# Reordering VectorE's work between the first two weight pairs of a fused decoder trunk's last matrix product, and forming one operand's low parts by an adding DMA

## The chip, the cores and the metric

The kernel runs on one core of a Trainium2 chip. The metric is the device time of one execution in microseconds (us). Before the change three runs took 1341.61, 1343.89 and 1345.63 us; their median is 1343.89 us. One execution was also recorded by the hardware profiler. Times within it are counted from the start of its span.

## The reference

One decoder layer over 1024 tokens of width 1024, all in float32. The change lies in the last part, the gated MLP's down projection, its residual and the final norm.

```python
def conv_ffn(xn, w_up, conv_w, conv_b, w_down):
    u = xn @ w_up
    upad = jnp.pad(u, ((0, 0), (CONV_WIDTH - 1, 0), (0, 0)))
    c = conv_b
    for j in range(CONV_WIDTH):
        c = c + upad[:, j:j + S] * conv_w[j]
    gate, val = jnp.split(c, 2, axis=-1)
    return (jax.nn.silu(gate) * val) @ w_down        # 2816 -> 1024

def reference(...):
    ...                                              # norm, two attentions, merge, residual
    xn = rmsnorm(x, norm_ffn_w[l])
    x = x + conv_ffn(xn, w_up[l], conv_w[l], conv_b[l], w_down[l])
    return rmsnorm(x, norm_final_w)
```

## The kernel before

**Three products for one.** Every float32 operand is split into a high part (a copy rounded to the format that TensorE reads, `F32R`) and a low part (the operand minus its high part). A product is made of high x high, high x low and low x high. ScalarE makes the high part (`nc.scalar.copy`), VectorE the low part (`tensor_tensor ... subtract`). For weights the tiles are `wh`/`wl` and `sh`/`sl`, for activations a tile `h<slot>` holds both parts side by side. `split` (L832) and `parts_h` (L1041) do this for activations.

**Down projection (`down`, L1110).** The hidden width 2816 is 22 chunks of 128. The first 6 go through a plain product (L1159). The next 8 and the last 8 are two groups, and each group is multiplied by a scheme with seven block products instead of eight: output rows m and m + 4 form a pair (four pairs, m = 0..3), the tokens are two halves of 512, and the operands are single blocks or sums of blocks of the weights (A11, A12, A22, S1 to S4) and of the activations (B11, B21, B22 and the sums T1 to T4). One block product (`product`, L906) is 12 TensorE instructions: four chunks k times three parts. Results gather in PSUM banks, tags `d` and `y`, four of each, and VectorE adds them into the output tile `x3` (`x` in the profile, `col(m, hf)` in the code).

**The second group, around the change.** The loop over m at L1279 makes for each pair, in this order on TensorE:

- P1 = A11 x B11 into a bank `y`. VectorE adds the bank into `col(m, 0)` (L1285) and leaves it as it is, since P6 and P7 gather on top of it.
- P2 = A12 x B21 into a bank `d`, added by `evac` (L1260), which also squares and weighs the finished block on ScalarE for the final norm (L1263, L1267).
- P7 = S3 x T3 of the pair before (`seventh`, L1275), onto that pair's `y`.
- P4 = A22 x T4 into a bank `d`, subtracted at L1292.
- P6 = S2 x T2 onto `y`, added at L1294. It may be written only after L1285 has read P1.

After the loop come `fifth` (with T1) and `third` (with B22), whose weight sums were stored in HBM (`sd`) and are read back, and then the final norm in pieces (`last_norm`, L1347).

**Weights of a pair** come by `second_pair` (L138): two loads on SyncE's queue into three rotating `raw` buffers, four sums on GpSimd (L148 to L151), a store of two of them, and three splits (L157), of A11/A12 and of S2/S3 (128x1024 each) and of A22 (128x512). `next_w(n)` hands out the next pair and makes sure that n are under way.

**Operands of the second group.** The list `more` (L1216) holds the steps in order: B11, B21, T4, T2, the four tiles `box` for the norm's sums, T3, T1, B22, four steps (k = 0..3) each. `prepare(n)` takes the next n steps. `read` loads a raw row block `hr` from HBM (L1034) and splits it; `ready` splits a difference that was formed earlier (`diffs`, L1201). Slots are `h14` to `h17` for T4, `h21, h25, h1, h5` for T2, `h20, h24, h0, h4` for T3, `h7, h9, h11, h13` for T1, `h6, h8, h10, h12` for B22.

A scheduler places the instructions on each engine's queue mostly in the order of the code; `tc.issue_after(i)` asks for a place behind instruction i on its engine. Each engine then works its queue in order.

Of the kernel before, what the change touches and what calls it, by code (L numbers as in the profile page):

```python
# [10 lines left out]
F32 = mybir.dt.float32  # L11
F32R = mybir.dt.float32r
AF = mybir.ActivationFunctionType
ALU = mybir.AluOpType
# [3 lines left out]
P = 128  # L18
# [4 lines left out]
H2 = 512  # L23
# [8 lines left out]
N2 = N1 + 8  # L32
# [12 lines left out]
class Trunk:  # L45
    def __init__(self, tc, ins, out):
        self.tc, self.nc = tc, tc.nc
        (self.xT, self.w_in, self.w_br, self.w_mix, self.w_up, self.w_dn,
         self.vecs_d, self.bias_d) = ins
        self.out = out  # L50
        self.uid = 0
        self.stores = []
        self.uw = self.w22 = self.behind = None
        self.pin, self.after = False, None
        self.hs, self.defer, self.late = {}, [], []

    def name(self, s):
# [80 lines left out]
    def second_pair(self, src, m):  # L138

        nc = self.nc  # L140
        raws = []
        for x in src:
            raws.append(self.tl(self.wp, [P, 8, P], "raw", bufs=RAW))
            nc.sync.dma_start(raws[-1], x)
        g, v = (r.rearrange("p (k a) c -> p a k c", a=2) for r in raws)
        sa, sb = (self.tl(self.sfp[0], [P, 2, 4, P], self.sfp[1]) for _ in range(2))
        tt = nc.gpsimd.tensor_tensor
        tt(sa[:, 0], v[:, 0], v[:, 1], ALU.add)  # L148
        tt(sb[:, 0], sa[:, 0], g[:, 0], ALU.subtract)
        tt(sb[:, 1], g[:, 0], v[:, 0], ALU.subtract)  # L150
        tt(sa[:, 1], g[:, 1], sb[:, 0], ALU.subtract)  # L151
        nc.sync.dma_start(self.sd[m], sa.rearrange("p a k c -> p (a k) c"))
        ops = {}
        for pool, h, l, x, names in ((self.wp, "wh", "wl", g, ("A11", "A12")), (self.uw, "sh", "sl", sb, ("S2", "S3")), (self.wp, "wh", "wl", v[:, 1:2], ("A22",))):
            hi = self.tl(pool, [P, len(names), 4, P], h, F32R)
            lo = self.tl(pool, [P, len(names), 4, P], l, F32R)
            self.made = nc.scalar.copy(hi, x), nc.vector.tensor_tensor(lo, x, hi.bitcast(F32), ALU.subtract)  # L157
            for i, name in enumerate(names):
                ops[name] = hi[:, i], lo[:, i]
        return ops  # L160

    def load_raw(self, src, nk):
# [875 lines left out]

        return self.tl(self.hp if i < HP else self.hpb, [P, 2, H2], f"h{i}", dt)

    def parts_h(self, src, i=None):  # L1041

        if i is None:
            i = self.nh % (HP + HPB)
            self.nh += 1
        h = self.slot(i, F32R)
        return self.split(h[:, 0], h[:, 1], src)

    def load_h(self, j, hf, eng=None):
# [60 lines left out]
    def down(self):  # L1110

        nc, tc = self.nc, self.tc
        with ExitStack() as ctx:
# [7 lines left out]
            tt = nc.vector.tensor_tensor  # L1121
            bank = lambda n: self.tl(psD, [P, H2], "dy"[n])
            x3 = xp.tile([P, KC, T], F32, name="x3")
            col = lambda m, hf: x3[:, m, hf * H2:(hf + 1) * H2]
# [20 lines left out]
            n = N1 // 2  # L1145
            for i, (m, c) in enumerate(self.pieces):
# [3 lines left out]
                w = [v[:, i % 2 * n:i % 2 * n + n] for v in w2]  # L1150
                lo = self.lo
                for hf in range(2):
# [3 lines left out]
                    for q, j in enumerate(js):  # L1156
                        h, l = self.hs[hf, j]
# [16 lines left out]
                if c == 1:  # L1174

                    for hf in range(m < 4, 2):
                        x = col(m, hf)
# [3 lines left out]
            for m in range(4):  # L1181
                wh, wl = self.next_w()
                y, ps = bank(1), pss[m, 0]
# [26 lines left out]
            def ready(n, k, i):  # L1210
                self.B["2" + n, k] = self.parts_h(raws[k][("T1", "T3", "T4", "T2").index(n)], i)

            def read(n, k, o, hf, i):
                self.B["2" + n, k] = self.parts_h(self.raw_h(N2 + 2 * k + o, hf), i)

            box = []  # L1216
            more = [lambda k=k: read("B11", k, 0, 0, old("T1", k)) for k in range(4)]
            more += [lambda k=k: read("B21", k, 1, 0, old("T2", k)) for k in range(4)]
            more += [lambda k=k: ready("T4", k, base + 8 + k) for k in range(4)]
            more += [lambda k=k: ready("T2", k, old("T4", k)) for k in range(4)]  # L1220
            more += [lambda: box.append(self.tl(self.hrp, [P, H2], "hr")) for _ in range(4)]
            more += [lambda k=k: ready("T3", k, old("T3", k)) for k in range(4)]
            more += [lambda k=k: ready("T1", k, base + 2 * k + 1) for k in range(4)]
            more += [lambda k=k: read("B22", k, 1, 1, base + 2 * k) for k in range(4)]

            def prepare(n):
                for _ in range(min(n, len(more))):
                    more.pop(0)()
# [3 lines left out]
            for m, y in enumerate(ys):  # L1232
                w = self.next_w()
# [5 lines left out]
                i = tt(col(m, 1), col(m, 1), y, ALU.add)  # L1239
# [7 lines left out]
                i = tt(col(m + 4, 0), col(m + 4, 0), ps, ALU.subtract)  # L1247
# [2 lines left out]
                self.product(y, w["S3"], "T3", first=False, skip=True)  # L1250
                for hf in range(2):
                    tt(col(m + 4, hf), col(m + 4, hf), y, ALU.add)
            prepare(20)
            q = H2 // 2
            seen = []

            def evac(ps, m, hf, a=0, b=H2, last=False):

                x = x3[:, m, hf * H2 + a:hf * H2 + b]
                tt(x, x, ps, ALU.add)  # L1260
                sum_ = box[hf][:, a:b]
                sq = box[2 + len(seen) % 2][:, a:b] if hf in seen else sum_
                self.square = nc.scalar.activation(sq, x, AF.Square)  # L1263
                if hf in seen and not last:
                    tt(sum_, sum_, sq, ALU.add)
                seen.append(hf)
                weigh = lambda: nc.scalar.mul(x, x, self.vecs[:, C_NO + m:C_NO + m + 1])  # L1267
                if last:
                    return sq, weigh
                weigh()  # L1270
# [3 lines left out]
            def seventh(m):  # L1274
                self.product(ys[m], ws[m]["S3"], "2T3", first=False, skip=True)  # L1275
                evac(ys[m], m + 4, 0)
                tt(col(m + 4, 1), col(m + 4, 1), ys[m], ALU.add)

            for m in range(4):  # L1279
                w = self.next_w()  # L1280
                ws.append(w)
                y, ps = bank(1), bank(0)
                ys.append(y)
                self.product(y, w["A11"], "2B11", skip=True, low_last=True)
                tt(col(m, 0), col(m, 0), y, ALU.add)  # L1285
                self.product(ps, w["A12"], "2B21")
                evac(ps, m, 0)
                if m:
                    seventh(m - 1)
                ps = bank(0)  # L1290
                self.product(ps, w["A22"], "2T4")
                tt(col(m + 4, 0), col(m + 4, 0), ps, ALU.subtract)  # L1292
                self.product(y, w["S2"], "2T2", first=False, skip=True)
                tt(col(m, 1), col(m, 1), y, ALU.add)  # L1294
                with ExitStack() as queue:
                    for i in self.made:
                        queue.enter_context(tc.issue_after(i.ins))
                    prepare(4 if m else 8)
            seventh(3)
            assert not more  # L1300
            tail = self.last_norm(psD, [box[0]], x3, 0, 0, H2, ((0, 2, nc.vector), (6, 8, nc.gpsimd), (2, 4, nc.vector), (4, 6, nc.vector)))
# [145 lines left out]
```

## Time and profile before

| | |
|---|---|
| median of three runs | 1343.89 us |
| the profiled execution | 1342.84 us |
| its span, first to last instruction | 1340.6 us |
| TensorE (PE) busy | 1319.9 us, 98% |
| VectorE (DVE) busy | 1069.3 us, 80% |
| ScalarE (ACT) busy | 621.2 us, 46% |
| GpSimd (POOL) busy | 497.0 us, 37% |
| mean granted TensorE clock | 0.997 |
| second group, 1247 to 1304 us: TensorE | 54.1 us of 57 busy |
| second group: VectorE | 53.7 us of 57 busy |

PE, DVE, ACT and POOL are the engines; SPq is SyncE's queue of DMA issues. A row of a timeline is start, duration, engine, line, operation, the tile written and the tiles read, their shapes and a count of like instructions that follow each other; in brackets stands the idle time before it and who ended it. Matmuls overlap, so the distance between two starts is what one costs, not its duration. `out<-in` names leave out buffer numbers, so all `h` slots read alike.

### The profile page before, as it was taken

The numbers are of one execution on the slowest core, as the hardware profiler recorded it, in microseconds if no ns is written. First come the engines' busy times: TensorE is split into PE (matmuls) and PEld (weight loads), VectorE is DVE, ScalarE is ACT, GpSimd is POOL, SyncE is SP. The second block draws the span as 40 slices with busy tenths as digits, with TensorE's granted clock in tenths as the row PEclk, the third lists the DMA queues.
The fourth block names the chain that finished last, engine by engine and source line by source line (L and its number), as shares of the span: only waits on it lengthen the run. The fifth ranks groups of instructions, "written<-read, shape, count | busy, mean of one in ns | idle before, by whom it ended". The sixth has DMA issues, their size and how long they took to land.

```text
span 1340.6 us, 17301 instructions
## 1 busy us (share of the span) xinstructions
PE 1319.9 (98%) x6264; PEld 1097.0 (82%) x6264; DVE 1069.3 (80%) x1605; ACT 621.2 (46%) x1019; POOL 497.0 (37%) x365
## 2 busy tenths in 40 slices
PE   8999999999999999999999999999999999999997
PEld 6888888888888777878888888888888888888787
DVE  8847775289889876465678999999999997978985
ACT  9432232276667765333444443444443444323454
POOL 0336553001102124651446555655565510215422
PEclk9999999999999999999999999999999999999998
DMA  7423443876553235334432222222222229671333
GB/s 258 145 107 143 156 158 141 246 182 186 144 135 124 97 119 203 141 110 157 126 110 95 78 95 79 94 68 90 90 85 80 85 82 337 214 263 63 112 124 126
DMA packets 63045, 182.64 MB, mean 136 GB/s; under 512 B 6896, under 2 KB 15216, under 8 KB 62960
## 3 DMA queue, kind: packets, MB, share of 16 engines
q1 hardware_dynamic: 51504, 164.13, 37.5%
q10 hardware_dynamic: 11456, 17.41, 3.6%
q8 instruction: 49, 0.80, 0.3%
q14 instruction: 36, 0.29, 0.1%
HBM read 130.66 MB, written 50.86 MB: 135 GB/s over the span
## 4 chain that ended last, share of the span: by engine, by line
PE 87%; POOL 4%; DVE 4%; DMA 3%; ACT 1%; issue 1%; POOLq 0%; SPq 0%; ACTq 0%; DVEq 0%
PE t L920 13%; PE t L921 13%; PE t L922 13%; PE g L209 3%; PE t L914 3%; PE g L210 3%; PE g L211 3%; PE sc L636 3%; PE y L1159 2%; PE d L1159 2%; DMA gr<-gd 2%; PE sc L211 2%; PE sc L209 2%; PE sc L210 2%; PE d L920 2%; PE d L921 2%
## 5 line engine op out<-in xcount | busy, mean ns | idle before, releaser
L1089 ACT ACTIVATE c<-us,vecs 128x512 f32<-128x512 f32 x80 | 61.3, 780 | 133.2 <-POOL us L1083 129.2
L1091 DVE SCALAR_TENSOR_TENSOR c<-us,vecs,c 128x512 f32<-128x512 f32 x160 | 110.4, 747 | 8.6 <-ACT c L1089 8.5
L1083 POOL TENSOR_TENSOR us<-us,rstd 128x1024 f32<-128x1024 f32 x38 | 99.7, 2643 | 4.5 <-DVE us L469 2.4
L128 DVE TENSOR_TENSOR sl<-sf,sh 128x1024 fp32r<-128x1024 f32 x62 | 87.6, 1415 | 11.5 <-ACT sh L127 11.5
L127 ACT CAST sh<-sf 128x1024 fp32r<-128x1024 f32 x62 | 63.3, 1048 | 60.2 <-PE t L921 43.7
L176 DVE TENSOR_TENSOR wl<-raw,wh 128x1024 fp32r<-128x1024 f32 (+2 forms) x46 | 55.7, 1210 | 31.8 <-ACT wh L174 20.2
L128 DVE TENSOR_TENSOR wl<-raw,wh 128x1024 fp32r<-128x1024 f32 (+1 forms) x35 | 76.3, 2180 | 3.7 <-ACT wh L127 3.6
L103 POOL TENSOR_TENSOR sf<-rv 128x512 f32<-128x512 f32 x30 | 41.3, 1378 | 100.9 <-DVE sl L128 57.8
L174 ACT CAST wh<-raw 128x1024 fp32r<-128x1024 f32 (+2 forms) x46 | 46.1, 1001 | 61.8 <-PE sc L210 30.5
L209 PE MATMUL g<-xh,wh 128*128 128x512 f32 x176 | 70.6, 401 | 0.1
L211 PE MATMUL g<-xh,wl 128*128 128x512 f32 x176 | 70.3, 400 | 0.0
L210 PE MATMUL g<-xl,wh 128*128 128x512 f32 x176 | 70.3, 399 | 0.0
L108 POOL TENSOR_TENSOR sf<-raw,rv 128x512 f32<-128x512 f32 x30 | 40.7, 1358 | 65.3 <-DVE sl L128 65.3
L619 POOL MEMSET aT<- 128x128 f32 x32 | 6.2, 206 | 151.6 <-PE t L665 101.3
L640 DVE CUSTOM_DVE_ANT_0 L<-sc,bias 128x128 f32<-128x128 f32 (+7 forms) x64 | 47.7, 751 | 17.0 <-PE sc L636 13.7
L641 ACT ACTIVATE L<-L,sm 128x128 f32<-128x128 f32 (+7 forms) x64 | 49.6, 778 | 20.0 <-DVE sm L640 17.3
L794 POOL TENSOR_TENSOR gr<-gr,rstd 128x1024 f32<-128x1024 f32 x16 | 40.6, 2540 | 42.5 <-DMA gr<-gd 42.3
L1093 ACT ACTIVATE c<-c 128x512 f32<-128x512 f32 x40 | 24.0, 599 | 60.7 <-DVE c L1091 60.7
L128 DVE TENSOR_TENSOR wl<-rv,wh 128x512 fp32r<-128x512 f32 x30 | 49.3, 1642 | 3.5 <-ACT wh L127 3.5
L636 PE MATMUL sc<-u,u 128*128 128x512 f32 (+2 forms) x192 | 49.8, 358 | 0.0
L211 PE MATMUL sc<-mh,wl 128*128 128x512 f32 x126 | 49.1, 390 | 0.5 <-DVE wl L176 0.5
L209 PE MATMUL sc<-mh,wh 128*128 128x512 f32 x126 | 49.0, 389 | 0.0
(527 smaller groups left out, 4400.3 us busy)
## 6 DMA issues: line engine op xcount, KB each, us to landing
u<-qd SPq DMA_DIRECT2D x72, 256.0 KB, 6.6
raw<-in_w_in SPq DMA_DIRECT2D x25, 512.0 KB, 4.2
raw<-in_w_up SPq DMA_DIRECT2D x23, 512.0 KB, 3.5
hr<-hd SPq DMA_DIRECT2D x46, 256.0 KB, 4.9
hd<-c SPq DMA_DIRECT2D x22, 512.0 KB, 2.6
rv<-in_w_up SPq DMA_DIRECT2D x21, 512.0 KB, 3.5
raw<-in_w_down SPq DMA_DIRECT2D x19, 512.0 KB, 4.2
gr<-gd SPq DMA_DIRECT2D x16, 512.0 KB, 3.7
```

The costliest lines, as they stand in the source:

```text
L127: i = nc.scalar.copy(hi, src)
L128: j = nc.vector.tensor_tensor(lo, src, hi.bitcast(F32), ALU.subtract)
L209: nc.tensor.matmul(ps, wh[:, kc + o, :], ah, start=first and n == 0, stop=False)
L210: nc.tensor.matmul(ps, wh[:, kc + o, :], al, start=False, stop=False)
L211: nc.tensor.matmul(ps, wl[:, kc + o, :], ah, start=False, stop=last and n == len(kcs) - 1)
L636: nc.tensor.matmul(sc[:, lo + n0:lo + n1], qs, k[c][part][:, n0:n1], start=part == 0, stop=part == 1)
L920: nc.tensor.matmul(ps, ah[:, k, :], bh, start=first and n == 0, stop=False, skip_group_check=skip)
L921: nc.tensor.matmul(ps, ah[:, k, :], bl, start=False, stop=False, skip_group_check=skip)
L922: i = nc.tensor.matmul(ps, al[:, k, :], bh, start=False, stop=last and n == len(ks) - 1, skip_group_check=skip)
L1083: (nc.vector if j == 0 else nc.gpsimd).tensor_tensor(u[:, 2:], u[:, 2:], self.rstd, ALU.mult)
L1089: nc.scalar.activation(c, u[:, o + 2:o + 2 + H2], AF.Identity, bias=self.vecs[:, C_CB + m:C_CB + m + 1], scale=col(m, 2))
L1091: nc.vector.scalar_tensor_tensor(c, u[:, o + k:o + k + H2], col(m, k), c, ALU.mult, ALU.add)
```

## The change

Four edits, all in the second group:

- `prepare(20)` ahead of the loop becomes `prepare(16)`: T2's splits no longer stand ahead of the loop. The `box` tiles are taken ahead of T2. Inside the loop, for m = 0, T2's splits are issued behind the addition of P1 (`issue_after`).
- The second pair is asked for (`ahead(1)`) behind that addition too, and its splits are queued behind it (`self.later`).
- After each pair four steps are prepared instead of eight after the first: T3, T1 and B22 follow pairs 0, 1 and 2.
- B22's low parts are formed in another way: ScalarE copies the high part and then multiplies it by -1 into the low part's place, and a DMA issued by GpSimd adds the raw rows `hr` onto it.

```diff
@@ second_pair
-            self.made = nc.scalar.copy(hi, x), nc.vector.tensor_tensor(lo, x, hi.bitcast(F32), ALU.subtract)
+            with self.tc.issue_after(self.later.ins) if self.later is not None else nullcontext():
+                self.made = nc.scalar.copy(hi, x), nc.vector.tensor_tensor(lo, x, hi.bitcast(F32), ALU.subtract)
...
+        self.later = None
         return ops
@@ parts_h
-    def parts_h(self, src, i=None):
+    def parts_h(self, src, i=None, adding=False):
...
+        if adding:
+            self.nc.scalar.copy(h[:, 0], src)
+            self.nc.scalar.mul(h[:, 1], h[:, 0].bitcast(F32), -1.0)
+            self.nc.gpsimd.dma_start(h[:, 1], src, accum_op=ALU.add)
+            return h[:, 0], h[:, 1]
         return self.split(h[:, 0], h[:, 1], src)
@@ down
-                self.B["2" + n, k] = self.parts_h(self.raw_h(N2 + 2 * k + o, hf), i)
+                self.B["2" + n, k] = self.parts_h(self.raw_h(N2 + 2 * k + o, hf), i, n == "B22")
...
+            more += [lambda: box.append(self.tl(self.hrp, [P, H2], "hr")) for _ in range(4)]
             more += [lambda k=k: ready("T2", k, old("T4", k)) for k in range(4)]
-            more += [lambda: box.append(self.tl(self.hrp, [P, H2], "hr")) for _ in range(4)]
...
-            prepare(20)
+            prepare(16)
...
-                w = self.next_w()
+                w = self.next_w(2 if m else 1)
...
-                tt(col(m, 0), col(m, 0), y, ALU.add)
+                i = tt(col(m, 0), col(m, 0), y, ALU.add)
+                if m == 0:
+                    with tc.issue_after(i.ins):
+                        prepare(4)
+                    self.later = i
+                    self.ahead(1)
...
-                    prepare(4 if m else 8)
+                    prepare(4)
```

What it does to the queues, first on VectorE at the start of the second group. Before, from T4's last low part (`h17`): T2's low parts, the second pair's A11/A12 (`wl_1903`) and S2/S3 (`sl_1905`), the addition of P1 (L1285), A22 (`wl_1907`), and then the additions of P2 and P4.

```order
L834 TENSOR_TENSOR h17_1889_10945<-h13_1817_10508,h17_1889_10945 128x512
L834 TENSOR_TENSOR h21_1890_10948<-h7_1811_10496,h21_1890_10948 128x512
L834 TENSOR_TENSOR h25_1891_10951<-h9_1813_10500,h25_1891_10951 128x512
L834 TENSOR_TENSOR h1_1892_10954<-h11_1815_10504,h1_1892_10954 128x512
L834 TENSOR_TENSOR h5_1893_10957<-h13_1817_10508,h5_1893_10957 128x512
L157 TENSOR_TENSOR wl_1903_10976<-raw_1898_10964,wh_1902_10975 128x1024
L157 TENSOR_TENSOR sl_1905_10980<-c_1901_10969,sh_1904_10979 128x1024
L1285 TENSOR_TENSOR x3_9784<-x3_9784,y_1908_10987 128x512
L157 TENSOR_TENSOR wl_1907_10984<-raw_1899_10966,wh_1906_10983 128x512
L1260 TENSOR_TENSOR x3_9784<-x3_9784,d_1909_10988 128x512
L1292 TENSOR_TENSOR x3_9784<-x3_9784,d_1910_11017 128x512
```

After the change, from the same row (lines are a few numbers higher, L1293 is the addition of P1, L1307 that of P6):

```order
L837 TENSOR_TENSOR h17_1889_10945<-h13_1817_10508,h17_1889_10945 128x512
L1293 TENSOR_TENSOR x3_9784<-x3_9784,y_1894_10952 128x512
L837 TENSOR_TENSOR h21_1896_10967<-h7_1811_10496,h21_1896_10967 128x512
L837 TENSOR_TENSOR h25_1897_10970<-h9_1813_10500,h25_1897_10970 128x512
L837 TENSOR_TENSOR h1_1898_10973<-h11_1815_10504,h1_1898_10973 128x512
L837 TENSOR_TENSOR h5_1899_10976<-h13_1817_10508,h5_1899_10976 128x512
L159 TENSOR_TENSOR wl_1905_10991<-raw_1900_10979,wh_1904_10990 128x1024
L159 TENSOR_TENSOR sl_1907_10995<-c_1903_10984,sh_1906_10994 128x1024
L159 TENSOR_TENSOR wl_1909_10999<-raw_1901_10981,wh_1908_10998 128x512
L1268 TENSOR_TENSOR x3_9784<-x3_9784,d_1895_10953 128x512
L1305 TENSOR_TENSOR x3_9784<-x3_9784,d_1910_11017 128x512
L1307 TENSOR_TENSOR x3_9784<-x3_9784,y_1894_10952 128x512
```

The addition of P1 moved from behind six rows (T2 and the second pair) to ahead of them, and the addition of P6 moved ahead of T3's first low parts.

TensorE at the same place, before, from the last instruction of P4 (`d_1910`): six instructions of the second pair's P1 (`y_1929`), then P6 of the first pair (`y_1908`).

```order
L922 MATMUL d_1910_11017<-h17_1889_10945,wl_1866_10823 128x512
L914 MATMUL y_1929_11091<-h18_1871_10898,wh_1902_10975 128x512 x2
L914 MATMUL y_1929_11091<-h22_1873_10903,wh_1902_10975 128x512 x2
L914 MATMUL y_1929_11091<-h26_1875_10908,wh_1902_10975 128x512 x2
L920 MATMUL y_1908_10987<-h21_1890_10948,sh_1863_10818 128x512
L921 MATMUL y_1908_10987<-h21_1890_10948,sh_1863_10818 128x512
L922 MATMUL y_1908_10987<-h21_1890_10948,sl_1864_10819 128x512
```

After, from the same row; the first pair's bank is now `y_1894`, and the second pair's P1 begins behind all twelve instructions of P6:

```order
L925 MATMUL d_1910_11017<-h17_1889_10945,wl_1866_10823 128x512
L923 MATMUL y_1894_10952<-h21_1896_10967,sh_1863_10818 128x512
L924 MATMUL y_1894_10952<-h21_1896_10967,sh_1863_10818 128x512
L925 MATMUL y_1894_10952<-h21_1896_10967,sl_1864_10819 128x512
L923 MATMUL y_1894_10952<-h25_1897_10970,sh_1863_10818 128x512
L924 MATMUL y_1894_10952<-h25_1897_10970,sh_1863_10818 128x512
L925 MATMUL y_1894_10952<-h25_1897_10970,sl_1864_10819 128x512
```

P6 moved ahead of the second pair's P1.

ScalarE around B22 (`h6, h8, h10, h12`), before:

```order
L833 CAST h6_1933_11168<-hr_1932_11166 128x512
L833 CAST h8_1935_11173<-hr_1934_11171 128x512
L833 CAST h10_1937_11178<-hr_1936_11176 128x512
L833 CAST h12_1939_11183<-hr_1938_11181 128x512
L157 CAST wh_1944_11197<-raw_1940_11186 128x1024
```

After, from the split of the fourth pair's A22 (`wh_1940`) to the first weights that are read back (`wh_1954`):

```order
L159 CAST wh_1940_11185<-raw_1933_11168 128x512
L1051 CAST h6_1947_11268<-hr_1946_11266 128x512
L1051 CAST h8_1949_11274<-hr_1948_11272 128x512
L1052 ACTIVATE h6_1947_11268<-h6_1947_11268 128x512
L1052 ACTIVATE h8_1949_11274<-h8_1949_11274 128x512
L1051 CAST h10_1951_11280<-hr_1950_11278 128x512
L1051 CAST h12_1953_11286<-hr_1952_11284 128x512
L1052 ACTIVATE h10_1951_11280<-h10_1951_11280 128x512
L1052 ACTIVATE h12_1953_11286<-h12_1953_11286 128x512
L177 CAST wh_1954_11290<-raw_1942_11189 128x1024
```

B22's high parts moved behind the fourth pair's weights, and four multiplications by -1 (L1052) joined them.

GpSimd at the end of the weight sums, after; before, the four DMA rows are not there:

```order
L152 TENSOR_TENSOR c_1934_11170<-raw_1932_11166,c_1935_11171 128x512
L1053 DMA h6_1947_11268<-hr_1946_11266 128x512
L1053 DMA h8_1949_11274<-hr_1948_11272 128x512
L1053 DMA h10_1951_11280<-hr_1950_11278 128x512
L1053 DMA h12_1953_11286<-hr_1952_11284 128x512
L232 TENSOR_TENSOR rs_1969_11438<-ms_1968_11436,mhalf_78 128x4
```

The four adding DMAs stand between the last weight sum and the first power of the final norm. SyncE's queue keeps its order.

More of the change, by code (lines that the diff above doesn't have):

```diff
@@ L156, in second_pair @@
             lo = self.tl(pool, [P, len(names), 4, P], l, F32R)
-            self.made = nc.scalar.copy(hi, x), nc.vector.tensor_tensor(lo, x, hi.bitcast(F32), ALU.subtract)
+            with self.tc.issue_after(self.later.ins) if self.later is not None else nullcontext():
+                self.made = nc.scalar.copy(hi, x), nc.vector.tensor_tensor(lo, x, hi.bitcast(F32), ALU.subtract)
             for i, name in enumerate(names):
                 ops[name] = hi[:, i], lo[:, i]
+        self.later = None
         return ops
```

## The prediction

> **What bounds the kernel now.** I read the page first, then TensorE's waits and the chain of waits in the stretch that the change touches, then the timelines of the engines there.
>
> ```profile
> span 1340.6 us, 17301 instructions
> PE 1319.9 (98%) x6264; PEld 1097.0 (82%) x6264; DVE 1069.3 (80%) x1605; ACT 621.2 (46%) x1019; POOL 497.0 (37%) x365
> ```
>
> TensorE is busy for 98% of the span, so only idle time of TensorE, or a longer tail behind it, can move the end. Its waits from 1236 us to the end (engine, tile and line, who was waited for, us in total, times, longest):
>
> ```profile
> PE y L920 <- DVE x L1285: 2.9, 1, 2.9
> PE d L235 <- POOL rs L229: 1.0, 1, 1.0
> ```
>
> The second belongs to the final norm, which the change leaves alone; the only other wait is shorter still. One wait of 2.9 us is left for it to win. The chain of waits shows what ended it (start, us, what):
>
> ```profile
> 1254.35 2.41 DVE h L834 x4
> 1256.76 1.14 DVE wl L157
> 1257.89 1.13 DVE sl L157
> 1259.03 0.61 DVE x L1285
> 1259.68 0.50 PE y L920
> ```
>
> TensorE wants to add P6 of pair 0 to bank y, but VectorE must first have added P1 out of that bank (L1285), and that addition stood behind T2's four low parts and the second pair's two wide low parts. The same in TensorE's timeline: P1 at 1246.88, P4 at 1252.33, six products of the next pair's P1 at 1255.26, the wait, P6 at 1259.68; the row of 1266.61 begins P7 of pair 0, that of 1280.22 P7 of pair 1, that of 1311.16 the first product with B22.
>
> ```profile
> 1246.88 1.98 PE L914 MATMUL y<-h,wh 128*128 128x512 f32 x8
> ...
> 1252.33 0.39 PE L920 MATMUL d<-h,wh 128*128 128x512 f32 x1
> ...
> 1255.26 1.53 PE L914 MATMUL y<-h,wh 128*128 128x512 f32 x6
> 1259.68 0.50 PE L920 MATMUL y<-h,sh 128*128 128x512 f32 x1 [2.89 <-DVE x L1285]
> ...
> 1266.61 0.39 PE L920 MATMUL y<-h,sh 128*128 128x512 f32 x1
> ...
> 1280.22 0.39 PE L920 MATMUL y<-h,sh 128*128 128x512 f32 x1
> ...
> 1311.16 0.49 PE L920 MATMUL d<-h,wh 128*128 128x512 f32 x1
> ```
>
> From 1246.88 to 1252.33 lie 24 products (P1 and P2), so one is issued every 0.227 us. Six from 1255.26 end their issue at 1256.62; the next came at 1259.68: 3.06 us of issue are lost. VectorE's timeline beside it:
>
> ```profile
> 1251.87 4.89 DVE L834 TENSOR_TENSOR h<-h,h 128x512 fp32r<-128x512 f32 x8
> 1256.68 1.21 DVE L157 TENSOR_TENSOR wl<-raw,wh 128x1024 fp32r<-128x1024 f32 x1
> 1257.82 1.21 DVE L157 TENSOR_TENSOR sl<-c,sh 128x1024 fp32r<-128x1024 f32 x1
> 1258.95 0.67 DVE L1285 TENSOR_TENSOR x<-x,y 128x512 f32<-128x512 f32 x1
> ...
> 1261.35 1.28 DVE L834 TENSOR_TENSOR h<-h,h 128x512 fp32r<-128x512 f32 x2
> ...
> 1263.34 7.30 DVE L834 TENSOR_TENSOR h<-h,h 128x512 fp32r<-128x512 f32 x6
> 1270.56 0.68 DVE L1285 TENSOR_TENSOR x<-x,y 128x512 f32<-128x512 f32 x1
> ```
>
> **The change part by part.** *The addition of P1 ahead of T2.* The eight low parts are T4's four, then T2's four, 0.60 us apart. With the addition between them it starts four steps after 1251.87, at 1254.27, and ends by 1254.94; P1 ended long before. P4 still ends its issue at 1255.26, so P6 can follow at once. T2's low parts come at 1254.87, 55.47, 56.07 and 56.67, each done 0.68 later; P6 wants them at 1255.49 and then every 0.68. Only the first is late, by about 0.1 us. P6, P1 and P2 of pair 1 are 36 products, 8.16 us: P7 of pair 0 comes up at 1255.26 + 0.1 + 8.16 = 1263.52, not 1266.61. That is a lead of 3.1 us. The second pair's wide low parts start at 1257.28, 0.6 later than before, and are done by 1259.6; P1's low half wants the first at 1259.9, so this edit costs nothing.
>
> *What is late next.* P7 needs T3's four low parts, which VectorE did at 1261.35 (two) and from 1263.34. In the new order the wide parts end their turn at 1259.55; four short steps follow (the second pair's A22 part and three additions), so T3's start at 1261.95. There they meet GpSimd, which sums the third pair's weights, started by a load that waits for the wide part on VectorE:
>
> ```profile
> 1257.92 0.33 SPq L144 DMA_DIRECT2D raw<-in_w_down  x1
> ```
>
> ```profile
> 1261.57 2.21 POOL L148 TENSOR_TENSOR c<-raw 128x512 f32<-128x512 f32 x1 [9.67 <-DVE x L1292]
> 1263.75 1.74 POOL L150 TENSOR_TENSOR c<-raw,raw 128x512 f32<-128x512 f32 x1
> ```
>
> The load went out 0.03 us after the wide part's end (1257.89); that end moves 0.6 us, and GpSimd's first sum with it, to 1262.17. In the old run six low parts beside GpSimd took 7.30 us instead of 3.6: low parts and sums went in turn, one low part for each sum. So T3's first two parts pass at 1261.95 and 1262.55 as the old pair at 1261.35 did, the third waits for the first sum (2.21 us after 1261.57, so about 1.2 after the second part frees the way at 1263.15), and is done at 1264.9; the fourth waits for the second sum, 1.15 us, and is done at about 1266.7. P7 wants the fourth at its eleventh product, 1263.52 + 2.27 = 1265.79. It loses 0.9 us, and the lead becomes 3.1 - 0.9 = 2.2 us.
>
> Who goes first matters here. Twice the second of two VectorE steps in a row overtook a sum that had already started: at 1261.95 (in the x2 row above), and at 1277.02, half a microsecond after GpSimd's start, at its plain 0.68 us:
>
> ```profile
> 1276.52 2.34 POOL L148 TENSOR_TENSOR c<-raw 128x512 f32<-128x512 f32 x1 [7.64 <-DMA raw<-in_w_down]
> 1277.02 0.68 DVE L1265 TENSOR_TENSOR hr<-hr,hr 128x512 f32<-128x512 f32 x1
> ```
>
> So I let T3's second part (1262.55) pass the sum of 1262.17 as well, and take 2.2 us. If the sum went first, every later part would stand one sum further back, 1.15 us: the fourth at 1267.85, the loss 2.0, the lead 1.1. If no sum got in the way, the lead would stay 3.1. Those are the ends.
>
> The Trainium skill ("SBUF — State Buffer", section "SBUF: two separate sides") says that of a VectorE operation with two SBUF inputs and a GpSimd operation that reads SBUF, whichever starts first holds the shared ports for its whole length; that would be the lead of 1.1 us. That they go in turn, the trace agrees; that the earlier start wins, the two overtaken sums do not bear out.
>
> *T1's operands a pair later, B22's low parts off VectorE.* VectorE had T1's four parts in the six from 1263.34, so the addition of pair 1's P1 moves from 1270.56 to about 1266.65. From there to the addition of its P6, which P7 of pair 1 waits for, the old run took 8.77 us, with one B22 part in between:
>
> ```profile
> 1277.73 1.68 DVE L834 TENSOR_TENSOR h<-hr,h 128x512 fp32r<-128x512 f32 x1
> 1279.33 0.68 DVE L1294 TENSOR_TENSOR x<-x,y 128x512 f32<-128x512 f32 x1
> 1279.93 4.58 DVE L834 TENSOR_TENSOR h<-hr,h 128x512 fp32r<-128x512 f32 x3
> ```
>
> Now two T1 parts stand there: 1266.65 + 8.77 + 1.7 = 1277.1, done by 1277.8. P7 of pair 1 comes at 1280.22 - 2.2 = 1278.0. It holds, with 0.2 us to spare. The B22 parts cost VectorE 1.68 + 4.58 = 6.3 us, but TensorE waited for none of them (its waits above), so taking them away is worth nothing by itself.
>
> *B22 by DMA.* ScalarE gets four multiplications by -1 more, and GpSimd issues four DMAs of 256 KB that add hr onto them.
>
> ```profile
> L1267 ACT ACTIVATE x<-x,vecs 128x512 f32<-128x512 f32 x7 | 4.9, 720 | 0.1
> ```
>
> ```profile
> hr<-hd SPq DMA_DIRECT2D x4, 256.0 KB, 4.5
> ```
>
> ScalarE's multiplications are 4 x 0.72 = 2.9 us. Before the casts stands the fourth pair's A22 cast, which needs P4 of pair 2, at about 1286 now; casts and multiplications are done from 1288.4 to 1291, and the next cast in the queue waits for a product of about 1291.6 anyway. TensorE wants the first low part right after 1311.16 - 2.2 = 1309.0 and the fourth at 1311.3. No row shows a DMA issued by GpSimd, nor one that adds. The nearest is the plain load of 256 KB, 4.5 us. Four of these one after the other end at 1288.4 + 18 = 1306.4, 4.9 us before the fourth is needed; overlapping, far earlier. So I take zero, and bound it by twice the row: 1288.4 + 36 = 1324.4, 13 us late. It can't gain: nobody waits earlier. GpSimd's next work behind the DMAs is the norm's power at about 1309.
>
> The Trainium skill ("DMA: Bandwidth & Descriptors", "Anatomy of one DMA — SWDGE (gpsimd) path") gives 2.0 us plus bytes over 436 GB/s for such a DMA, by my estimate 2.6 us each, 1298.8 for all four; the sum would be the same. No run here shows it yet.
>
> **The sum.** 3.06 us of lost issue come back, 0.9 goes to T3's low parts: 2.2 us. The profiled execution took 1342.84 us around its span of 1340.6; it would take 1340.6. The median of the three runs is 1343.89, 1.05 above it, and from the median I get 1341.7. The runs spread from 1341.61 to 1345.63, so less than 0.3% (4.0 us) can't be told from no change; the whole stall is smaller than that.
>
> **The rivals.** *GpSimd's sum goes ahead of T3's second part:* lead 1.1 us, 1342.8, still no change that could be told. For it: the sum's start lies 0.4 us ahead of the part's. Against it: the two overtaken sums above. It is also what the ports' rule in the Trainium skill ("SBUF — State Buffer", "SBUF: two separate sides") would give.
>
> *The wait comes back at P7 of pair 1.* The 0.2 us to spare rests on when the last pair's sums start. Their load goes out when the third pair's four sums are done, near 1270 now, and at 3.65 us from issue to first sum (1257.92 to 1261.57) they begin near 1274, as the old ones of 1276.52 did beside the same steps. A load a microsecond quicker puts one or two sums more among VectorE's steps, 1.15 us each, and P7 waits for the addition of P6: the lead shrinks by 1 to 2.2 us, 1342.7 to 1343.9, no change. For it: VectorE has hardly a gap there. Against it: the old run had the same sums in the same place.
>
> *Slower: B22's DMAs land after TensorE wants them.* The point is 1311.3 for the fourth; from 1288.4 that is 5.7 us for each if they go one behind the other. Each microsecond more per DMA costs four. At twice the plain load (9 us) TensorE waits 13 us and the time is 1341.7 + 13 = 1354.8. For it: they read the target, add and write, which no row prices, and GpSimd must issue each while VectorE keeps working on SBUF. Against: five microseconds each is already more than the plain load, and they can overlap. The Trainium skill ("SBUF — State Buffer", "SBUF: two separate sides") warns that a DMA issued by GpSimd waits for its descriptors while VectorE holds the shared ports; that would make this rival likelier. In the rows, a sum beside VectorE's steps took 2.34 us at most (1276.52); held up as long as that each, the four would still end before 1311.
>
> That the change doesn't do what it says is no rival: the order shows the addition ahead of T2 and P6 ahead of the next P1.
>
> **How the numbers follow.** Forecast (a lead of about 2.2 us, up to 3.1): 0.51. The sum goes first: 0.13. The wait returns: 0.14. DMAs late: 0.16. Something that no row shows, either way: 0.06. Low end: all 3.1 us and a session 2 us quick like the fastest run, 1338.8. High end: nothing gained and the slowest run's 1.7, 1345.6. That leaves out the late DMAs and a little of the rest. By the 0.3%: the forecast and the two rivals with a smaller lead lie within it, except where the runs' spread carries them over, 0.15 faster; the late DMAs and half of the unknown make 0.19 slower; 0.66 within.
>
> **What would show it.** Right: the 2.9 us wait on the addition is gone; the first y product of P6 follows P4 without a gap; TensorE waits about 0.9 us at P7 of pair 0 for a low part of T3; four DMAs from GpSimd landing before 1309. Wrong: a wait of y on the addition of P6 at about 1278; a wait of d near 1309 on a DMA; a tail longer than the 9 us after the last product.

## The result, and the profile after

The changed kernel took 1338.97 us in the median (1338.0 to 1341.4), the kernel before 1343.77 beside it: a ratio of 0.9969, with a 95% interval of 0.9959 to 0.9979. That is 2.8 to 5.5 us, where the prediction had 2.2. It lies within the range, 0.2 us above its low end. The ratio is just past the 0.3%, on the side that had been given 0.15, though its interval reaches back to 0.2%. The profiled execution took 1338.85 us. The page, and TensorE's waits from 1236 us on:

```profile
span 1337.1 us, 17312 instructions
PE 1319.5 (99%) x6264; PEld 1096.2 (82%) x6264; DVE 1062.9 (79%) x1601; ACT 623.2 (47%) x1023; POOL 500.9 (37%) x369
```

```profile
PE d L238 <- POOL rs L232: 1.0, 1, 1.0
PE d L924 <- DVE h L837: 0.2, 1, 0.2
PE d L1374 <- ACT hr L1271: 0.2, 1, 0.2
```

The wait of 2.9 us is gone; the one new wait, 0.2 us, is P4's for a low part of T4. TensorE's timeline of the stretch (the rows are P1, P4's first two products, P6's first two, and the first of P7 of pair 0):

```profile
1246.37 1.98 PE L917 MATMUL y<-h,wh 128*128 128x512 f32 x8
...
1251.81 0.39 PE L923 MATMUL d<-h,wh 128*128 128x512 f32 x1
1252.38 0.50 PE L924 MATMUL d<-h,wh 128*128 128x512 f32 x1 [0.19 <-DVE h L837]
...
1255.01 0.39 PE L923 MATMUL y<-h,sh 128*128 128x512 f32 x1
1255.39 0.50 PE L924 MATMUL y<-h,sh 128*128 128x512 f32 x1
...
1263.47 0.39 PE L923 MATMUL y<-h,sh 128*128 128x512 f32 x1
```

From P1's first product to P7's first, which is the same work in both kernels, it was 1266.61 - 1246.88 = 19.73 us and is 1263.47 - 1246.37 = 17.10. So 2.63 of the 3.5 us between the two spans lie in this stretch, 0.5 us lie ahead of it, where nothing was changed, and the rest at the very end. VectorE and GpSimd beside it:

```profile
1251.65 2.49 DVE L837 TENSOR_TENSOR h<-h,h 128x512 fp32r<-128x512 f32 x4
1254.06 0.68 DVE L1293 TENSOR_TENSOR x<-x,y 128x512 f32<-128x512 f32 x1
1254.66 2.49 DVE L837 TENSOR_TENSOR h<-h,h 128x512 fp32r<-128x512 f32 x4
...
1261.73 2.48 DVE L837 TENSOR_TENSOR h<-h,h 128x512 fp32r<-128x512 f32 x4
1264.14 0.67 DVE L1293 TENSOR_TENSOR x<-x,y 128x512 f32<-128x512 f32 x1
```

```profile
1262.11 3.26 POOL L149 TENSOR_TENSOR c<-raw 128x512 f32<-128x512 f32 x1 [10.42 <-DMA raw<-in_w_down]
...
1286.15 2.92 POOL L1053 DMA_DIRECT2D h<-hr  x3 [3.25 <-DVE wl L159]
1291.84 0.89 POOL L1053 DMA_DIRECT2D h<-hr  x1 [2.77 <-ACT wh L177]
```

The addition of P1 (1254.06) stands between T4's parts and T2's. T3's four parts (1261.73) ran at 0.60 us each although GpSimd's sum started at 1262.11: the sum waited, 3.26 us instead of the 1.3 it takes alone. The adding DMAs went out from 1286.15 on. Two questions stay: why the medians lie 4.8 us apart and the stretch only 2.63, and why T3's parts weren't held up.

### The profile page after: what moved, and what is told of

The parts are those of the page before. It is cut to its first block, busy times and chain, and to the rows that moved or that the text cites. A ratio compares the mean times of both kernels' runs of the same rounds, so it can differ in the third digit from the quotient of the medians.

```text
span 1337.1 us, 17312 instructions
## 1 busy us (share of the span) xinstructions
PE 1319.5 (99%) x6264; PEld 1096.2 (82%) x6264; DVE 1062.9 (79%) x1601; ACT 623.2 (47%) x1023; POOL 500.9 (37%) x369
## 4 chain that ended last, share of the span: by engine, by line
PE 87%; POOL 4%; DMA 3%; DVE 3%; ACT 1%; issue 1%; POOLq 0%; SPq 0%; ACTq 0%; DVEq 0%
PE t L924 13%; PE t L925 13%; PE t L923 13%; PE t L917 3%; PE sc L639 3%; PE g L212 3%; PE g L213 3%; PE g L214 3%; PE y L1167 2%; PE d L1167 2%; DMA gr<-gd 2%; PE sc L214 2%; PE sc L213 2%; PE sc L212 2%; PE d L924 2%; PE d L923 2%
```

## The experiments

Times are medians, each with its ratio to the kernel before that ran beside it. "P1 to P7" is the distance just used.

**The kernel before, against itself.** No edit.

> The kernel before, unchanged, against itself. The result showed 3.5 us between two profiled spans and 4.8 us between two medians, while the lines of the changed stretch give 2.65 us. Theory A (the change gives back the wait for the addition of P1 and nothing else): a ratio of 1.000 with an interval of some 0.1% to either side; a second profile shows the same wait of 2.9 us at P6 of pair 0, and its TensorE starts stand apart from the first profile's by 0.5 us or so in stretches that no change touches (the first 13 us, the merge stage near 520 to 590 us, the last 3 us), which would make the 0.85 us beyond 2.65 scatter. Theory B (the change also speeds something outside the stretch): the two profiles of the same kernel agree within 0.1 us in those stretches, and the 0.85 us is the change's own.

1342.68 us, ratio 1.000 (0.9991 to 1.001). The old wait was there, but P1 to P7 took 21.33 us, 1.6 more than in the profile that the prediction was made from. TensorE's granted clock shows where. The row of 1255 to 1264 us (length; busy time of PE, PEld, DVE, ACT, POOL; granted clock; DMA share; GB/s) of the first profile and of this one:

```profile
1255.00:1264.00 9.00, 6.11 (x27) 4.72 (x26) 8.89 (x13) 6.03 (x11) 2.43 (x2) 1.00 0.48 153
```

```profile
1255.00:1264.00 9.00, 6.54 (x22) 5.25 (x23) 7.54 (x11) 3.99 (x8) 4.55 (x3) 0.81 0.40 117
```

Ahead of the stretch the two profiles of one kernel stand 2.2 us apart (P1 began at 1246.88 and at 1244.68). That is more scatter than theory A had put there, and the 0.5 us between the kernels lies within it.

**The kernel before once more, for its profile.** Two theories are named from here on. Theory E: a long wait of TensorE costs its length and, in most executions, half speed for the products behind it. Theory F: the low clock has nothing to do with the wait, which costs its length alone.

> The kernel before once more, for its profile alone. Of three profiles with its wait of 2.9 us two had a clock of 0.81 in the stretch behind it, one had 1.00. Theory E: 0.8 is the commoner case, and P1 to P7 takes 21.3 us here or, less often, 19.7, hardly anything between. Theory F: 19.7.

P1 to P7: 21.42 us, clock 0.81. TensorE behind the wait:

```profile
1257.26 0.50 PE L920 MATMUL y<-h,sh 128*128 128x512 f32 x1 [2.93 <-DVE x L1285]
1257.60 0.40 PE L921 MATMUL y<-h,sh 128*128 128x512 f32 x1
...
1259.02 0.63 PE L920 MATMUL y<-h,sh 128*128 128x512 f32 x1
1259.44 0.63 PE L921 MATMUL y<-h,sh 128*128 128x512 f32 x1
1259.87 0.63 PE L922 MATMUL y<-h,sl 128*128 128x512 f32 x1
```

Some 1.3 us behind the wait the products stand 0.43 us apart instead of 0.227, for seven of them here, 1.7 us more than in the first profile that no idle time shows. The clock row says the same: 0.81 over 9 us is short of 1.00 by 1.7 us, which is 3.4 us at half speed.

**T2's parts ahead of the addition again** (a wait of 2 us):

```diff
-            prepare(16)
+            prepare(20)
...
-                    with tc.issue_after(i.ins):
-                        prepare(4)
```

> The changed kernel with one edit undone: T2's four low parts stand ahead of the addition of P1 again; the second pair's wide parts stay behind it. The addition moves from 1254.06 to 1256.47 and ends at 1257.1; P6 goes straight after P4 in TensorE's order, so TensorE waits about 2.1 us for it, with nothing in between. P1 to P7 takes 17.1 + 1.8 = 18.9 us (the 0.3 us of small waits for T2's parts go). By theory F that is all: 1.8 us slower than the changed kernel. By theory E the wait is long enough to slow the products behind it in some executions: up to 1.6 us more, a profile with a clock under 1.00 between 1255 and 1264, and times further apart.

1341.18 us, 0.9982 (0.9971 to 0.9992); the changed kernel beside it, below, took 1339.44. P1 to P7: 18.99, the predicted 18.9. The wait and the clock:

```profile
1257.15 0.50 PE L923 MATMUL y<-h,sh 128*128 128x512 f32 x1 [2.03 <-DVE x L1293]
```

```profile
1255.00:1264.00 9.00, 6.97 (x31) 5.67 (x31) 9.00 (x14) 3.99 (x7) 1.84 (x1) 1.00 0.46 142
```

This one edit is worth 1.7 us. The wait of 2.0 us brought no slow products in this profile. Of the 11 executions, the three with a mean clock of 0.996 took 1342.0 to 1343.2 us and the four at 0.998 or 0.999 took 1338.1 to 1340.9, so in some it may have; no profile shows one of those.

**A wait of 4 us.** On top of that edit:

```diff
-                self.B["2" + n, k] = self.parts_h(raws[k][("T1", "T3", "T4", "T2").index(n)], i)
+                x = raws[k][("T1", "T3", "T4", "T2").index(n)]
+                h, l = self.B["2" + n, k] = self.parts_h(x, i)
+                for _ in range(2 if n == "T2" else 0):
+                    nc.vector.tensor_tensor(l, x, h.bitcast(F32), ALU.subtract)
```

> The changed kernel with T2's parts ahead of the addition of P1 again, and each of those four low parts formed three times over (the same subtraction, the same values), which puts 8 steps, 4.8 us, more ahead of the addition. TensorE's order then has 12 products of the next pair between P4 and P6; they end near 1257.7, the addition near 1261.9: a wait of about 4.2 us in one piece, and 21.6 us from P1 to P7 (two products of the next P4 come ahead as well). Theory F (a wait costs its length): that is all, 2.2 us slower than the kernel with T2's parts ahead and a wait of 2.0 us. Theory E (the granted clock falls behind a long wait): products 0.43 us apart behind the wait, a clock under 1.00 between 1255 and 1270, up to 1.7 us more from P1 to P7, and 3 to 4 us slower than the kernel with the wait of 2.0 us.

1346.48 us, 1.0026 (1.0014 to 1.0037). P1 to P7: 23.96 us, or 23.51 without the two products of the next P4 (0.45 us) that lie in it here.

```profile
1261.76 0.79 PE L923 MATMUL y<-h,sh 128*128 128x512 f32 x1 [4.12 <-DVE x L1296]
1262.35 0.63 PE L924 MATMUL y<-h,sh 128*128 128x512 f32 x1
1262.77 0.63 PE L925 MATMUL y<-h,sl 128*128 128x512 f32 x1
...
1266.61 0.53 PE L925 MATMUL y<-h,sl 128*128 128x512 f32 x1
```

```profile
1255.00:1264.00 9.00, 4.88 (x17) 3.68 (x16) 9.00 (x15) 2.43 (x5) 0.00 (x0) 0.78 0.07 20
1264.00:1270.00 6.00, 6.00 (x22) 4.79 (x21) 4.59 (x6) 1.35 (x2) 3.36 (x3) 0.76 0.58 171
```

All 12 products of P6 ran at about 0.43 us each. Against the kernel with the wait of 2.0 us the median is 5.3 us higher: 2.1 of longer wait, some 2.3 of slow products, and about 1 us of a new wait for T3's parts at P7, which neither theory had. The two clock rows are short of 1.00 by 2.0 and 1.4 us together, 6.8 us at half speed. Theory E holds, theory F falls.

**The changed kernel again.** No edit.

> The changed kernel again, on the chip that runs the three others of this set. Two more profiles of a kernel with the old wait (the kernel before again, and the DMA part alone) showed a granted clock of 0.81 between 1255 and 1264 us, with products 0.43 us apart behind the wait instead of 0.227, and 21.3 and 21.4 us from P1 to P7 of pair 0; the profile that the prediction was made from showed 1.00 and 19.73. Theory E (a long wait costs its length and, in most executions, half speed for the next products, 1.6 us more): without the wait the clock stays 1.00 in that stretch in every profile, P1 to P7 takes 17.1 us, and the times lie closer together than those of before. Theory F (the 0.81 is scatter that has nothing to do with the wait): it shows here as well.

1339.44 us (1338.5 to 1340.1), 0.9967 (0.9954 to 0.9979). P1 to P7: 16.94, clock:

```profile
1255.00:1264.00 9.00, 9.00 (x40) 7.06 (x39) 9.00 (x14) 4.06 (x7) 1.07 (x1) 1.00 0.50 151
```

All eight profiles of the runs here that have no wait of 1 us or more between P1 and P7 show 1.00 in that row; of the four with the wait of 2.9 us (the kernel before three times, and the DMA part alone, below), three show 0.81. The mean clock of every execution on record points the same way: 0.9965 in the mean over the 73 of the kernel before that ran beside the runs here, 0.9978 over the 39 of the changed kernel and of four variants without such a wait. The difference, 0.0013 of 1340 us, is 1.7 us; this is an estimate, since each clock is recorded to 0.001 and is a mean over the whole span.

**The DMA part alone**, on the kernel before (with the `adding` branch of `parts_h` as in the change):

```diff
-                self.B["2" + n, k] = self.parts_h(self.raw_h(N2 + 2 * k + o, hf), i)
+                self.B["2" + n, k] = self.parts_h(self.raw_h(N2 + 2 * k + o, hf), i, n == "B22")
```

> The kernel before, with one part of the change alone: B22's low parts by the adding DMAs; the order on VectorE is as before (T2's parts and the second pair's wide parts ahead of the addition of P1, T1's operands after pair 0). Theory A: a ratio of 1.000 (within 0.1%); the wait of 2.9 us at P6 of pair 0 stays. Theory B: 1 to 2 us faster than before.

1341.84 us, 0.9987 (0.9979 to 0.9996). The wait of 2.9 us stays, P1 to P7 takes 21.40 us, clock 0.81: TensorE gains nothing in the stretch. The time is still 1.3 us lower, just past what theory A allowed and within theory B's 1 to 2 us; against the kernel before in its own run (1342.68, above) it is 0.8 us lower. The interval, 0.04% to 0.21%, holds both theories, so the time does not decide between them. The next run asks the other way round.

**All but the DMA part:**

```diff
-                self.B["2" + n, k] = self.parts_h(self.raw_h(N2 + 2 * k + o, hf), i, n == "B22")
+                self.B["2" + n, k] = self.parts_h(self.raw_h(N2 + 2 * k + o, hf), i)
```

> The changed kernel, but B22's low parts formed by VectorE as before (four steps more on VectorE, no multiplications by -1, no adding DMAs). Theory A (only the order counts, the DMA part is worth nothing): the same as the changed kernel, a ratio to before of 0.9965 to 0.998 (2.7 to 4.7 us); VectorE's four parts fall between 1285 and 1290, where it idles 1.7 and 2.0 us now, so no wait of TensorE follows. Theory B (taking 6.3 us off VectorE brings part of the gain): 1 us or more slower than the changed kernel, with a wait on VectorE after 1285.

1338.44 us, 0.9965 (0.9953 to 0.9978); P1 to P7 16.94; TensorE waits for VectorE nowhere behind 1246. The order alone has the whole gain, and taking the DMA part out of the changed kernel costs nothing: theory B of this run falls. What the DMA part does for the kernel before, alone, stays open.

**The adding DMAs ten microseconds later:**

```diff
-                    for i in self.made:
+                    for i in self.made if m < 3 else [self.square]:
                         queue.enter_context(tc.issue_after(i.ins))
-                    prepare(4)
+                    prepare(4 if m != 2 else 0)
```

> The changed kernel with B22's casts, multiplications and adding DMAs prepared after the last pair instead of after the third, so that the first DMA goes out near 1297 instead of 1286; the addition of the last P6 and a weight split change places on VectorE besides. TensorE wants the first low part at 1308.5 and the fourth at 1310.6. In the trace after, the four DMAs took 3.9 to 6.4 us from issue to landing and three were under way at a time, the fourth going out 3.6 us behind the third. By these rows the last lands near 1307: no wait, and the time of the changed kernel. By the prediction's price (4.5 us each, one behind the other) the fourth lands at 1315, TensorE waits about 4 us for it, and the run is that much slower.

1338.51 us, 0.9961 (0.995 to 0.9973), no wait for a DMA. GpSimd's issues, and the median from issue to landing:

```profile
1297.72 1.08 POOL L1053 DMA_DIRECT2D h<-hr  x1 [14.02 <-DVE hr L1273]
1299.28 1.75 POOL L1053 DMA_DIRECT2D h<-hr  x2 [0.48 <-ACT h L1052]
1301.84 0.89 POOL L1053 DMA_DIRECT2D h<-hr  x1 [0.80 <-ACT h L1052]
```

```profile
h<-hr POOLq DMA_DIRECT2D x4, 256.0 KB, 3.6
```

The slowest took 4.3 us, so the last landed by 1306.1, ahead of TensorE. They overlap; a price of 4.5 us each in a row is out.

**The addition of P6 amid T3's parts** (`behind(n)` prepares n steps as the code did before, behind the pair's last split):

```diff
...
+                if m == 0:
+                    behind(1)
                 tt(col(m, 1), col(m, 1), y, ALU.add)
+                behind(3 if m == 0 else 4)
```

> The changed kernel with one step of VectorE moved by 1.8 us: the addition of P6 of pair 0 (it reads a PSUM bank) stands behind the first of T3's low parts instead of ahead of all four. This asks why T3's parts passed GpSimd's sum without a stop, where the prediction had taken 0.9 us for it. Theory C (a run of VectorE steps on SBUF keeps the ports from step to step, and a sum gets in only where VectorE reads PSUM or pauses; from then on they go in turn): the first sum runs beside the moved addition, 1262.1 to 1263.4; T3's second, third and fourth parts end near 1264.0, 1265.8 and 1267.6, each of 1.8 us, and TensorE waits 0.7 us for the third and 1.2 us more for the fourth at P7 of pair 0: about 1.9 us slower than the changed kernel. Theory D (VectorE always goes first): all four parts at 0.6 us, no wait at P7, the same time as the changed kernel within 0.2 us.

1340.88 us, 0.998 (0.9971 to 0.9989): 1.9 us over the changed kernel's 1338.97. From P7's first product to the next P1's first, the traces have 10.02 us here and 8.16 there, the same 1.9 us. VectorE, GpSimd and P7 on TensorE:

```profile
1261.48 0.68 DVE L837 TENSOR_TENSOR h<-h,h 128x512 fp32r<-128x512 f32 x1
1262.09 0.68 DVE L1315 TENSOR_TENSOR x<-x,y 128x512 f32<-128x512 f32 x1
1262.68 5.05 DVE L837 TENSOR_TENSOR h<-h,h 128x512 fp32r<-128x512 f32 x3
```

```profile
1262.50 1.29 POOL L149 TENSOR_TENSOR c<-raw 128x512 f32<-128x512 f32 x1 [10.46 <-DMA raw<-in_w_down]
```

```profile
1266.10 0.50 PE L924 MATMUL y<-h,sh 128*128 128x512 f32 x1 [0.55 <-DVE h L837]
...
1267.79 0.50 PE L924 MATMUL y<-h,sh 128*128 128x512 f32 x1 [0.72 <-DVE h L837]
```

The sum came while VectorE read PSUM, went through in 1.29 us, and from there T3's three parts took 1.7 us each (5.05 us). Theory C holds, D falls.

**T1's operands after pair 0 again:**

```diff
-                    prepare(4)
+                    prepare(4 if m else 8)
```

> The changed kernel with T1's operands prepared after pair 0 again, directly behind T3's. VectorE then has eight low parts in a row from 1261.73, and GpSimd's first sum comes at 1262.1. Theory C (a run of steps on SBUF keeps the ports until VectorE reads PSUM): all eight at 0.6 us, and the sum takes 5.5 to 6 us, until the addition of the next P1 at 1266.5 lets it in. The prediction's rule (they go in turn): T1's parts take 1.7 us each, as four of the six did in the profile before, and the addition of pair 1's P1 moves to 1270. For the time both give the same as the changed kernel within 0.3 us, since T1's place was put at no cost.

1339.85 us, 0.997 (0.9959 to 0.9982).

```profile
1261.54 4.89 DVE L837 TENSOR_TENSOR h<-h,h 128x512 fp32r<-128x512 f32 x8
1266.36 0.67 DVE L1293 TENSOR_TENSOR x<-x,y 128x512 f32<-128x512 f32 x1
```

```profile
1261.98 5.61 POOL L149 TENSOR_TENSOR c<-raw 128x512 f32<-128x512 f32 x1 [10.49 <-DMA raw<-in_w_down]
```

Eight parts in a row held the sum off for 4.3 us, until the addition read PSUM. Theory C again. T1's place costs nothing that the time shows.

**The second pair's splits not held back:**

```diff
-                w = self.next_w(2 if m else 1)
+                w = self.next_w()
...
-                    self.later = i
-                    self.ahead(1)
```

> The changed kernel with another edit undone: the second pair's splits aren't held behind the addition of P1. On VectorE the part of S2/S3 then stands ahead of the addition and the parts of A11/A12 and A22 between T2's four. From the trace after, the addition ends near 1255.9 and T2's parts near 1256.5, 1258.2, 1258.8 and 1260.0; TensorE waits some 0.9 us for the addition and then for the parts, four short waits of 2.4 to 2.7 us in all, and P1 to P7 takes about 19.6 us. My theory (this edit carries as much as the one on T2): the whole gain in the trace goes, though without one long wait the clock stays 1.00, so the time stays 1 to 2 us under before's. The rival (the addition of P1 alone carries the gain): P1 to P7 under 18.2 us, no more than 1 us slower than the changed kernel.

1341.77 us, 0.9989 (0.998 to 0.9998), 2.3 us over the changed kernel beside it. P1 to P7: 19.41 (19.6 expected), in short waits, with the clock at 1.00. The rival is out: moving the addition needs this edit as much as the one on T2.

**A try at a better order:** the two additions that close the first group behind the second pair's splits.

```diff
-                for hf in range(2):
-                    tt(col(m + 4, hf), col(m + 4, hf), y, ALU.add)
+                if m < 3:
+                    for hf in range(2):
+                        tt(col(m + 4, hf), col(m + 4, hf), y, ALU.add)
...
+                    with tc.issue_after(self.made[1].ins):
+                        for hf in range(2):
+                            tt(col(7, hf), col(7, hf), last, ALU.add)
```

> The changed kernel with the two additions that close the first group (its last bank y) moved from ahead of T4's low parts to behind the second pair's splits. T4's parts, the addition of P1 and T2's parts then start 1.2 us earlier, and the small waits that the trace after still has there (0.36 at P4's second product, 0.11 behind it, 0.26 in P6) go. P1 to P7 takes 16.5 us instead of 17.1 and 16.95; the time is 0.5 us under the changed kernel's, too little to tell from it. The rival (the additions are wanted early, or what comes behind moves into a new wait): P1 to P7 stays at 17, or a wait appears at P7.

1338.11 us, 0.9965 (0.9953 to 0.9978): the changed kernel's time. P1 to P7 is 16.87, not 16.5: T4's parts began earlier and met GpSimd's last sum.

```profile
1249.70 3.58 DVE L837 TENSOR_TENSOR h<-h,h 128x512 fp32r<-128x512 f32 x4
```

```profile
1249.31 1.62 POOL L152 TENSOR_TENSOR c<-raw,c 128x512 f32<-128x512 f32 x1
```

3.58 us instead of 2.49. The two additions read PSUM and had been the right filler beside that sum.

## Why the prediction held, and where its steps were off

*The wait at P6, 3.06 us: right in kind, too small.* It is gone, and P6 follows P4. But "only idle time of TensorE, or a longer tail behind it, can move the end" left the clock out: the wait cost 1.6 to 1.7 us more in three of four profiles with it, as slow products behind it, and the profile that I worked from was the fourth. This is the term that was mis-sized: 3.06 where the mean over the four is 3.06 + 0.75 x 1.65 = 4.3. I had not looked at the granted clock behind the wait, where the profile at hand showed 1.00.

*P6 without a gap, 0.1 us for T2's first part: 0.3.* The product that waits starts late, and the next one 0.11 us later than usual. P4 lost another 0.3 to T4's first part (1252.38), which I hadn't priced. Together they make the lead 2.63 in this profile, not 3.1.

*T3's parts and GpSimd's sums, 0.9 us: nothing.* The step that failed is "low parts and sums went in turn", taken to hold from the second part on. They go in turn only once a sum has got in, and a run of parts doesn't let it in. The old run's six parts went in turn because the addition of P6, which reads PSUM, stood among T3's (at 1262.73, between the two rows of parts). The upper end I gave, a lead without loss, is what came. The rival with a lead of 1.1, by the rule of the Trainium skill ("SBUF — State Buffer", "SBUF: two separate sides") that the earlier start holds the ports for its whole length, was out here; it held where the sum started during a PSUM read, as in the run with the addition amid T3's parts, where the sum of 1262.50 took its plain 1.29 us and the part that began at 1262.68 took 1.66.

*P7 of pair 1, 0.2 us to spare.* The addition of P6 of pair 1 ended at 1275.3, P7 began at 1277.07: 1.7 us to spare. The wait did not come back.

*B22's DMAs, nothing.* Right: the last went out at 1291.84 and none took over 6.4 us to land, so all were there by 1298.2, where I had allowed 1306.4 and TensorE came at 1308.3.

Together: the distance from P1 to P7 is 21.0 us in the mean over the four profiles with the wait of 2.9 us (19.73, 21.33, 21.42, 21.40) and 17.0 over the two of the changed kernel. That is 4.0 us, where 2.2 had been forecast; if nearly every execution has the slow products, as the mean clocks suggest, it is 4.4. The medians differ by 4.8 us beside the first result and by 3.5 in the repeat (1342.96 and 1339.44), and the ratios give 4.2 and 4.4. So the stretch carries the gain within the scatter. Some 0.45 us more lies outside the span (below), but the kernel without the adding DMAs gained as much without it.

That the time fell inside the range was in part luck. The low end, 1338.8, was a lead of 3.1 us and 2 us for a quick session. The session was not quick (1343.77 for the kernel before, against 1343.89); the slow products, which the sum didn't have, and the 0.9 us for T3's parts, which wasn't lost, came to about those 2 us.

## What to carry to other kernels

Price a wait of TensorE by its length and by the clock in the microseconds behind it, from more than one profile; here a wait near 3 us cost half as much again. Where VectorE and GpSimd both read SBUF, as the low parts and the sums do here, a string of VectorE steps without a pause or a PSUM read passes a waiting sum whole, so place PSUM-reading additions where a sum should get in, and not among steps that TensorE waits for. Moving one step forward pays in full only when everything that stood ahead of it moves behind it: with one of the two edits undone, 2.0 us of the stretch were lost again, with the other 2.5.

## What the runs showed of the hardware

- Behind a wait of 2.0 us the granted clock stayed 1.00 (one profile); behind 2.9 us it fell in three of four, with seven or eight products at 0.43 us; behind 4.1 us all 12 of P6 ran so. By the clock rows each of the three lost 1.7 us, 3.4 us at half speed, and the wait of 4.1 us cost twice that. The Trainium skill ("TensorE: Matmul & The Clock Gate", "What's actually happening") has the clock at half after an idle window of some 3.4 us that runs freely. The half speed agrees; that a shorter wait of 2.9 us suffices is not what the page says.
- GpSimd's sum was held 4.3 us by eight VectorE steps in a row, seven of which started after the sum.
- An adding DMA of 256 KB took 3.3 to 8.0 us from issue to landing over all runs, 3.9 to 6.4 in the first profile of the changed kernel. In every kernel with these DMAs the time exceeds the span by 1.74 to 1.85 us, in every one without by 2.18 to 2.30. Where these 0.45 us go, and the rest of the 1.3 us of the kernel with the DMA part alone, stays open: the kernel with all but the DMA part was no slower than the changed one.
